# Reworked seams between the stages of a decoder layer, and one more down group by block products

## The chip, the cores and the metric

The kernel runs on one core of a Trainium2 chip. The metric is the device time of one execution in microseconds (us). A core has TensorE (matrix products; PE in the profile, its weight loads PEld), VectorE (DVE), ScalarE (ACT), GpSimd (POOL) and SyncE (SP). The engines run their own instruction queues in order and wait for each other by semaphores; the sequencers of SP, ACT and POOL also issue the transfers (DMA) between the large memory (HBM) and the on-chip memory (SBUF). TensorE adds its results up in PSUM, eight banks of 512 fp32 columns.

## The reference

One layer of a decoder trunk, 512 tokens, width 2048: a normed input goes through gated linear attention (GLA, four heads), then a squared-ReLU MLP of width 8192, then a sigmoid gate times a projection of a per-layer embedding, and a final norm. All in fp32.

```python
u = rmsnorm(h, norm_mix);   h = h + gla_mixer(u, ...)           # w_in, chunked recurrence, w_out
h = h + square(relu(rmsnorm(h, norm_mlp) @ w_up)) @ w_down      # 2048 -> 8192 -> 2048
gate = sigmoid(rmsnorm(h, norm_ple) @ w_ple_gate)
h = h + gate * (p @ w_ple_proj)
return rmsnorm(h, norm_final)
```

## The kernel before

**Products.** Every large product is done in split fp32: each operand is a high part in the fast format fp32r (a cast on ScalarE) and a low part (value minus high part, on VectorE), and a product is three matmuls, high*high, high*low and low*high (`mm3`, lines 147 to 151, or the same inside `chunk`, lines 819 to 822). Most of the kernel's matmuls take a stationary 128x128 tile and 512 moving columns.

**Stages in order of time.** The GLA input projections and the attention (to about 690 us), the output projection `wo` (to 840), the up product (to 1500), the embedding projection (to about 1545), the down product (to about 2237), the gate product and the final norm.

**Block products.** The up product and part of the down product use a scheme of seven block products instead of eight. Weights and activations are split in two along the contraction, and each again in halves (256 tokens, 128 columns); `chunk_sums` (line 796) loads 512 KB of weights into a buffer `raw` with eight places and forms three sums there with three VectorE operations (L801, L804, L805); `chunk` (line 808) then makes high parts (L811) and low parts (L813) of seven places at a time, twice, and runs 2 x 7 x 3 = 42 matmuls of 256 columns. `combine` (line 825) puts the seven results together from PSUM in a wide buffer `e` (tag "w", of which there is one) by one ScalarE copy and five VectorE operations. A plain chunk (`plain_chunk`, line 882) does the same 512 KB of weights with 4 x 2 x 3 = 24 matmuls of 512 columns, one cast and one subtraction.

**Up stage.** 32 groups g of 256 hidden columns, four chunks each (k4 = 0 to 3). After the first chunk of the next group, `hidden` (line 838) combines, applies relu and square on ScalarE (L840, L841) and stores the result to `z_d` by two transfers on GpSimd's queue (L843).

**Down stage.** The 32 row chunks come in five slices of 4, 3, 3, 3, 3 chunks. In every slice eight output groups g run over the slice's chunks and add their sum to the residual `h_d` (load L847, additions L861 or L892, store L855; in the last slice one more multiplication by `f2`, L854). Groups 0, 3 and 7 are plain, the others use block products. `build` (line 896) makes the operands of one chunk, twice: it loads a pair of hidden tiles from `z_d` into a load buffer, forms three differences (L872 to L874) in a spare tile, and splits both the tiles and the differences into four slots (L871, L875, L876, L877). It is called at a slice's group 0, chunk by chunk, and for one chunk of the next slice after group 2.

**Buffers.** `wpool` has tags raw (3 buffers: incoming weights, the `pp` tiles of the embedding projection, and `u_late`), whi and wlo (4 each) and ld (2). `spool` has 34 slots of 4 KB, which hold all operands; up operands take 28, a slice of three chunks 24. `mpool` has single buffers.

**Seams.** In the output projection, `evac_out` (line 731) adds the residual, scales it into `u`, squares it and stores it; for the pairs kp = 0 to 4 of 128-row blocks it also makes the up operands at once. For kp = 5 and 6 the scaled copy goes into `u_late`, a tile of tag raw, and the operands of 5, 6, 7 are made after the loop (line 756). Then the first up weights are summed (line 966). At the start of the down stage the embedding projection runs in four parts (`project_embedding`, line 932), each after a `build`.

**Order.** The program's order is only a priority: a planner in the compiler simulates the program and puts each instruction into its engine's queue when, by its own account, it is ready and its buffer is free. `keep_in_program_order` on L801 restricts that for the first weight sum. Weights are all loaded on SyncE's queue, and hidden tiles and residuals on GpSimd's.

## Time and profile before

| | |
|---|---|
| times of three runs | 2417.47, 2419.46, 2421.09 us, median 2419.46 |
| profiled execution | 2423.99 us, its span from first to last instruction 2422.2 us |
| TensorE busy | 2361.6 us (97%), weight loads 2136.3 us (88%) |
| VectorE, ScalarE, GpSimd busy | 1690.2 (70%), 977.5 (40%), 152.5 us (6%) |
| mean granted TensorE clock | 0.984 |
| DMA | 341.09 MB, mean 141 GB/s |
| chain that ended last | PE 78%, issue 8%, DVE 5%, DMA 4% |

The page's strip of 40 slices (60.6 us each) shows TensorE at 9 tenths or more except in the first slice (7), the one from 787 (8), the one from 1514 (8) and the last (8). Busy time of a pipelined matmul is modelled, so the step from one matmul's start to the next one's is the better measure of its cost.

### The profile page before, as it was taken

How to read it: one execution, taken by the hardware profiler on the slowest of the kernel's cores; microseconds unless marked ns; L12 is line 12 of the kernel's file. 1: busy time of each engine (PE TensorE's matmuls, PEld its weight loads, DVE VectorE, ACT ScalarE, POOL GpSimd, SP SyncE). 2: the span in 40 equal slices, each digit the busy share in tenths (PEclk: the TensorE clock that was granted, in tenths of full speed). 3: DMA queues.
4: the chain of work that ended last, by engine and by line, in shares of the span. 5: the costliest groups of instructions: out<-in, count | busy, mean ns of one | idle time of the engine just before them, and what ended most of it. 6: DMA issues, size and time to landing. Idle time of an engine off the chain costs nothing.

```text
span 2422.2 us, 36477 instructions
## 1 busy us (share of the span) xinstructions
PE 2361.6 (97%) x14778; PEld 2136.3 (88%) x14778; DVE 1690.2 (70%) x2579; ACT 977.5 (40%) x1216; POOL 152.5 (6%) x282
## 2 busy tenths in 40 slices
PE   7999999999999899999999999899999999999998
PEld 6888888888878699999999998699898989899887
DVE  5654736547464588888888888578887888878435
ACT  4433424324332344444444446334433334434333
POOL 2000000000000000000000000000101010100000
PEclk8999999999999899999999999899999999999999
DMA  8333323332433344444444444545555565655433
GB/s 252 97 88 94 87 79 96 95 94 85 127 130 113 122 124 146 132 131 131 132 131 131 131 131 142 184 149 170 191 179 195 187 203 178 215 191 190 149 114 113
DMA packets 247753, 341.09 MB, mean 141 GB/s; under 512 B 13732, under 2 KB 202336, under 8 KB 247584
## 3 DMA queue, kind: packets, MB, share of 16 engines
q1 hardware_dynamic: 213072, 228.68, 31.0%
q0 software_dynamic: 30240, 105.75, 12.6%
q10 hardware_dynamic: 4272, 4.33, 0.6%
q8 instruction: 115, 1.88, 0.3%
q14 instruction: 54, 0.44, 0.1%
HBM read 281.05 MB, written 57.67 MB: 140 GB/s over the span
## 4 chain that ended last, share of the span: by engine, by line
PE 78%; issue 8%; DVE 5%; DMA 4%; ACT 1%; POOL 0%; ACTq 0%; DVEq 0%; POOLq 0%
PE ps_up L822 9%; PE ps_up L819 9%; PE ps_up L821 9%; PE ps_d L821 5%; PE ps_d L819 5%; PE ps_d L822 4%; DMA z<-z_d 3%; PE ps_wo L151 2%; PE ps_v L149 2%; PE ps_wo L149 2%; PE ps_v L150 2%; PE ps_og L150 2%; PE ps_v L151 2%; PE ps_og L149 2%; PE ps_og L151 2%
## 5 line engine op out<-in xcount | busy, mean ns | idle before, releaser
L811 ACT CAST whi_up<-raw_up 128x896 fp32r<-128x896 f32 x256 | 239.8, 940 | 317.5 <-PE ps_up L821 309.5
L813 DVE TENSOR_TENSOR wlo_up<-raw_up,whi_up 128x896 fp32r<-128x896 f32 x256 | 277.7, 1087 | 92.9 <-ACT whi_up L811 92.9
L819 PE MATMUL ps_up<-XS,whi_up 128*128 128x256 f32 x1024 | 290.4, 284 | 0.0
L821 PE MATMUL ps_up<-XS,whi_up 128*128 128x256 f32 x1024 | 290.4, 284 | 0.0
L822 PE MATMUL ps_up<-XS,wlo_up 128*128 128x256 f32 x1024 | 290.0, 284 | 0.0
L811 ACT CAST whi_d<-raw_dn 128x896 fp32r<-128x896 f32 x160 | 149.0, 942 | 241.1 <-PE ps_d L821 141.8
L819 PE MATMUL ps_up<-XA,whi_up 128*128 128x256 f32 x768 | 218.6, 285 | 3.7 <-ACT whi_up L811 3.7
L822 PE MATMUL ps_up<-XA,wlo_up 128*128 128x256 f32 x768 | 218.1, 284 | 0.5 <-DVE wlo_up L813 0.5
L821 PE MATMUL ps_up<-XA,whi_up 128*128 128x256 f32 x768 | 217.8, 284 | 0.0
L813 DVE TENSOR_TENSOR wlo_d<-raw_dn,whi_d 128x896 fp32r<-128x896 f32 x160 | 172.9, 1087 | 35.6 <-ACT whi_d L811 34.8
L819 PEld LDWEIGHTS ps_up<-XS,whi_up 128*128 128x128 f32 x1024 | 197.4, 193 | 0.0
L821 PEld LDWEIGHTS ps_up<-XS,whi_up 128*128 128x128 f32 x1024 | 197.3, 193 | 0.0
L822 PEld LDWEIGHTS ps_up<-XS,wlo_up 128*128 128x128 f32 x1024 | 197.1, 193 | 0.0
L821 PE MATMUL ps_d<-Zdl,whi_d 128*128 128x256 f32 x640 | 181.1, 283 | 0.0
L819 PE MATMUL ps_d<-Zdh,whi_d 128*128 128x256 f32 x640 | 181.1, 283 | 0.0
L822 PE MATMUL ps_d<-Zdh,wlo_d 128*128 128x256 f32 x640 | 181.1, 283 | 0.0
L150 PE MATMUL ps_d<-Zl,whi_d 128*128 128x512 f32 x384 | 151.9, 396 | 5.0 <-DVE Zl L876 5.0
L149 PE MATMUL ps_d<-Zh,whi_d 128*128 128x512 f32 x384 | 151.7, 395 | 3.9 <-ACT whi_d L139 2.2
L151 PE MATMUL ps_d<-Zh,wlo_d 128*128 128x512 f32 x384 | 151.5, 394 | 0.5 <-DVE wlo_d L141 0.5
L819 PEld LDWEIGHTS ps_up<-XA,whi_up 128*128 128x128 f32 x768 | 147.9, 193 | 4.2 <-ACT whi_up L811 3.9
L822 PEld LDWEIGHTS ps_up<-XA,wlo_up 128*128 128x128 f32 x768 | 148.0, 193 | 0.9 <-DVE wlo_up L813 0.8
L821 PEld LDWEIGHTS ps_up<-XA,whi_up 128*128 128x128 f32 x768 | 148.0, 193 | 0.2 <-issue 0.2
(345 smaller groups left out, 6057.9 us busy)
## 6 DMA issues: line engine op xcount, KB each, us to landing
raw_up<-in_w_up SPq DMA_DIRECT2D x128, 512.0 KB, 3.8
raw_dn<-in_w_down SPq DMA_DIRECT2D x80, 512.0 KB, 3.7
raw_d<-in_w_down SPq DMA_DIRECT2D x48, 512.0 KB, 3.8
h<-h_d POOLq DMA_DIRECT2D x40, 512.0 KB, 4.6
h_d<-h POOLq DMA_DIRECT2D x40, 512.0 KB, 3.0
raw_v<-in_gla_w_in SPq DMA_DIRECT2D x32, 512.0 KB, 3.8
raw_og<-in_gla_w_in SPq DMA_DIRECT2D x32, 512.0 KB, 3.7
raw_wo<-in_gla_w_out SPq DMA_DIRECT2D x32, 512.0 KB, 3.4
```

The lines of the kernel that those rows point to most:

```text
L149: nc.tensor.matmul(ps, lhsT=wa[0], rhs=wb[0], start=first, stop=False)
L150: nc.tensor.matmul(ps, lhsT=wa[0], rhs=wb[1], start=False, stop=False)
L151: nc.tensor.matmul(ps, lhsT=wa[1], rhs=wb[0], start=False, stop=last)
L811: nc.scalar.copy(hi[:, 1:8, :], raw[:, q_, 1:8, :])
L813: nc.vector.tensor_tensor(out=lo[:, 1:8, :], in0=raw[:, q_, 1:8, :], in1=hi[:, 1:8, :].bitcast(F32), op=ALU.subtract)
L819: nc.tensor.matmul(dst, lhsT=hi[:, wb, :], rhs=xh, start=first and q_ == 0 and half == 0, stop=False)
L821: nc.tensor.matmul(dst, lhsT=hi[:, wb, :], rhs=xl, start=False, stop=False)
L822: nc.tensor.matmul(dst, lhsT=lo[:, wb, :], rhs=xh, start=False, stop=last and q_ == 1 and (b == 3 or half == 1))
```

## The change

- `PLAIN` becomes (0, 7): group 3 of every slice is done by block products.
- Up stage: after `hidden`, `hidden_sums` forms the four differences of the hidden tile in the free half of `e` and stores them to a new buffer in HBM, `zd_d`. The two steps are taken one per chunk (`todo.pop(0)()`), no longer both at once.
- Down stage: `split` loads hidden tiles, or their stored differences, straight into the slot of the low part, casts the high part from it and subtracts in place. `build_to` does this for the tiles and `build_sums_to` for the differences, at separate times: tiles of the next slice after groups 2 and 6, differences after group 7 and during group 1.
- The embedding projection's four parts stand behind the four plain chunks of the first slice's group 0, and its `pp` tiles use the load buffers, of which there is one more (tag "ld2").
- Output projection: the scaled copies of kp 5 and 6 are written over the residual tile after it is stored; no `u_late`. The first up weights are loaded and summed after block i = 13. Square and scaling change places.
- x is loaded one block earlier. `f2` shares the single buffer of `acc2`.

```diff
-PLAIN = (0, 3, 7)
+PLAIN = (0, 7)
...
+    zd_d = dram.tile([NG, P, 4, HT], F32, name="zd_d")
...
     x_load(1)
+    x_load(2)
...
-                if ready % 2 == 0 and ready // 2 + 1 < NK // 2:
-                    x_load(ready // 2 + 1)
+                if ready % 2 == 0 and ready // 2 + 2 < NK // 2:
+                    x_load(ready // 2 + 2)
...
+    def load2(shape, name):
+        return mpool.tile(shape, F32, tag="ld2", name=name)
...
+    def scale_out(i, h):
+        nc.vector.scalar_tensor_tensor(
+            out=late["u"][:, i % 2, :], in0=h, scalar=vec("norm_mlp", i), in1=rb, op0=ALU.mult, op1=ALU.mult)
...
-            late["x"] = load([P, 2, T], f"xres_{kp}")
+            late["x"] = (load2 if kp == 5 else load)([P, 2, T], f"xres_{kp}")
...
-            if kp == 5:
-                late["s"] = wtile([P, 2, 2, T], "raw", "u_late")
             if kp in (5, 6):
-                late["u"] = late["s"][:, kp - 5, :, :]
+                late["u"] = late["x"]
...
-        nc.vector.scalar_tensor_tensor(
-            out=late["u"][:, i % 2, :], in0=h, scalar=vec("norm_mlp", i), in1=rb, op0=ALU.mult, op1=ALU.mult)
         add_squares(h, f"mlp_{i}", i == 0)
+        if kp not in (5, 6):
+            scale_out(i, h)
         if i % 2:
             nc.gpsimd.dma_start(h_d[kp], late["x"])
+            if kp in (5, 6):
+                for j in range(2):
+                    scale_out(i - 1 + j, late["x"][:, j, :])
+            if i == 13:
+                first_raw.append(raw_of(0))
...
-        bcast(ft, f2, "f2")
+        F2.append(mpool.tile([P, T], F32, tag="acc2", name="f2"))
+        bcast(ft, F2[0], "f2")
...
+    def hidden_sums(g, e):
+
+        for o, x, y in ((4, 2, 3), (5, 3, 1), (6, 2, 5), (7, 0, 6)):
+            nc.vector.tensor_tensor(out=e[:, o, :], in0=e[:, x, :], in1=e[:, y, :], op=ALU.subtract)
+        nc.gpsimd.dma_start(zd_d[g], e[:, 4:8, :])
...
-    def hidden_operands(kp, u, d):
...
+    def split(src, kp, name):
+
+        h, l = (slot([P, 4, HT], f"Z{name}{n}_{kp}", F32R) for n in ("h", "l"))
+        nc.gpsimd.dma_start(l.bitcast(F32), src)
+        nc.scalar.copy(h, l.bitcast(F32))
+        nc.vector.tensor_tensor(out=l, in0=l.bitcast(F32), in1=h.bitcast(F32), op=ALU.subtract)
+        return h, l
...
     def build_to(n):
+
         while built[0] < min(n, NG // 2):
-            build(built[0])
+            for kp in (2 * built[0], 2 * built[0] + 1):
+                u = split(z_d[kp].rearrange("p k (h t) -> p (k h) t", h=2), kp, "u")
...
+    def build_sums_to(n):
+        while built[1] < min(n, NG // 2):
+            for kp in (2 * built[1], 2 * built[1] + 1):
+                d = split(zd_d[kp], kp, "d")
+                ZOPS[kp][:4] = [(d[0][:, o, :], d[1][:, o, :]) for o in range(4)]
+            built[1] += 1
...
-            o = wtile([P, 2, 512], "raw", f"pp_{gi}_{t2}")
+            o = (load2 if (2 * gi + t2) % 3 == 2 else load)([P, 2, 512], f"pp_{gi}_{t2}")
...
-    raw_next = raw_of(0)
+    raw_next = first_raw[0]
...
-            if s_ == 0 and g == 0 and first:
-                for i in range(4):
-                    build_to(i // 2 + 1)
-                    project_embedding(i)
             if g == 0:
                 build_to(k4 + 1)
+            if g == 1:
+                build_sums_to(k4 + 1)
...
                 plain_chunk(ps, k4, g, first, last, f"{name}_{k4}")
+                if s_ == 0 and g == 0:
+                    flush()
+                    build_to(min(k4 + 2, end))
+                    project_embedding(k4)
+                    build_sums_to(k4 + 1)
...
-            if g == 2 and last and 8 * (SLICES[s_] + 1) <= 34:
-                build_to(end + 1)
+            if last and end < NG // 2:
+                if g == 2 and SLICES[s_] == 3:
+                    build_to(end + 2)
+                if g == 6:
+                    build_to(end + 3)
+                if g == 7:
+                    build_sums_to(end + 1)
         if todo and not first:
-            flush()
+            todo.pop(0)()
```

## Rows read from the trace of the kernel before

**Rows 1.** Busy time by stretch (from:to, length, engines, granted clock, DMA share, GB/s).
```profile
45.00:60.00 15.00, 8.13 (x27) 5.73 (x26) 8.59 (x11) 7.18 (x21) 3.39 (x5) 0.66 0.72 215
785.00:800.00 15.00, 9.92 (x29) 7.19 (x28) 7.95 (x12) 4.15 (x6) 1.28 (x2) 0.66 0.41 139
840.00:855.00 15.00, 8.27 (x40) 7.67 (x39) 14.97 (x28) 6.78 (x10) 1.33 (x2) 0.66 0.33 105
1500.00:1550.00 50.00, 35.67 (x114) 26.13 (x113) 30.38 (x38) 26.68 (x34) 4.29 (x8) 0.80 0.64 212
1720.00:1740.00 20.00, 17.20 (x86) 14.32 (x85) 17.14 (x26) 7.56 (x8) 2.12 (x4) 0.91 0.49 174
```
**Rows 2.** TensorE in order of time (start us, us), a plain and a block-product group.
```profile
1557.08 0.39 PE L150 MATMUL ps_d<-Zl,whi_d 128*128 128x512 f32 x1
1557.31 0.39 PE L151 MATMUL ps_d<-Zh,wlo_d 128*128 128x512 f32 x1
...
1590.29 0.28 PE L819 MATMUL ps_d<-Zdh,whi_d 128*128 128x256 f32 x1
1590.41 0.28 PE L821 MATMUL ps_d<-Zdl,whi_d 128*128 128x256 f32 x1
```
**Rows 3.** SyncE's queue in order of time, 30 to 60 us.
```profile
33.22 14.87 SPq L137 DMA_DIRECT2D raw_v<-in_gla_w_in  x3
48.14 2.01 SPq L244 DMA_DIRECT2D x<-in_x  x3
```
**Rows 4.** SyncE's queue from 1478, and line 822 (first and last start us).
```profile
1480.34 44.25 SPq L137 DMA_DIRECT2D raw_wp<-in_w_ple_proj  x4
...
L822 PE MATMUL ps_up<-XA,wlo_up x12: 283/283/385, 1491.3 to 1500.4; 128*128 128x256 f32 x12
...
L822 PE MATMUL ps_d<-Zh,wlo_d x6: 283/283/283, 1570.0 to 1574.7; 128*128 128x256 f32 x6
```
**Rows 5.** ScalarE in order of time, 785 to 792 us.
```profile
790.81 1.99 ACT L139 CAST whi_wo<-raw_wo 128x1024 fp32r<-128x1024 f32 x2
```
**Rows 6.** VectorE in order of time, 838 to 845 us (idle before in brackets).
```profile
839.61 1.37 DVE L745 TENSOR_TENSOR xres<-ps_wo,xres 128x512 f32<-128x512 f32 x2 [10.06 <-PE ps_wo L151]
...
844.82 0.68 DVE L801 TENSOR_TENSOR raw_up<-raw_up 128x512 f32<-128x512 f32 x1
```
**Rows 7.** TensorE in order of time, 843 to 848 us.
```profile
847.86 0.58 PE L819 MATMUL ps_up<-XA,whi_up 128*128 128x256 f32 x1 [2.60 <-ACT whi_up L811]
```
**Rows 8.** VectorE in order of time in the last slice, 2183 to 2188 us.
```profile
2183.64 0.68 DVE L834 TENSOR_TENSOR e_dn<-ps_d,e_dn 128x512 f32<-128x512 f32 x1
2184.24 0.41 DVE L835 TENSOR_TENSOR e_dn<-ps_d,e_dn 128x256 f32<-128x256 f32 x1
2184.57 1.28 DVE L861 TENSOR_TENSOR h<-h,e_dn 128x512 f32<-128x512 f32 x2
2185.78 1.08 DVE L813 TENSOR_TENSOR wlo_d<-raw_dn,whi_d 128x896 fp32r<-128x896 f32 x1
2186.78 1.22 DVE L854 TENSOR_TENSOR h<-h,f 128x1024 f32<-128x1024 f32 x1
2187.91 0.69 DVE L801 TENSOR_TENSOR raw_dn<-raw_dn 128x512 f32<-128x512 f32 x1
```
**Rows 9.** An up group's wide buffer by engine; transfers (KB, us to landing).
```profile
992.67 0.37 ACT L829 COPY e_up<-ps_up 128x256 f32<-128x256 f32 x1
...
1000.27 1.14 POOL L843 DMA_DIRECT2D z_d<-e_up  x2 [19.01 <-ACT e_up L841]
...
z_d<-e_up POOLq DMA_DIRECT2D x64, 256.0 KB, 2.8
...
h_d<-xres POOLq DMA_DIRECT2D x8, 512.0 KB, 2.9
```
**Rows 10.** Lines that write acc2 and read f2 (ns min/median/max, first to last start us).
```profile
L1037 DVE TENSOR_TENSOR acc<-acc,sq_ple x15: 683/685/694, 2136.7 to 2252.2; 128x512 f32<-128x512 f32 x15
...
L854 DVE TENSOR_TENSOR h<-h,f x8: 1218/1218/1224, 2117.9 to 2237.7; 128x1024 f32<-128x1024 f32 x8
```

More of the change, by code (lines that the diff above doesn't have):

```diff
@@ L725, in operands, with chunk_sums, raw_of @@
         return ops
+    w_up = a["w_up"].rearrange("o k c -> (o k) c")
+    w_dn = a["w_down"].rearrange("o k c -> (o k) c")
+    B11, T1, T3, B22, B21, T2, T4 = range(1, 8)
+    PRODUCTS = ((A11, B11), (R2, T2), (S3, T3), (S1, T1), (A12, B21), (R4, B22), (A22, T4))
+    BANK = ((0, 0), (0, 1), (1, 0), (1, 1), (2, 0), (2, 1), (3, 0))
+    def chunk_sums(w, k4, g, name):
+        raw = wtile([P, 2, 8, P], "raw", f"raw_{name}")
+        rows = raw.rearrange("p q (k b n) c -> p (q k) b (n c)", k=2, b=2)
+        nc.sync.dma_start(rows[:, :, 0, :], w_rows(w, 4 * k4, 4, 256 * g, 256))
+        tc.keep_in_program_order(nc.vector.tensor_tensor(
+            out=raw[:, :, 2:4, :], in0=raw[:, :, 1:5:3, :], in1=raw[:, :, 0:1, :].broadcast_to([P, 2, 2, P]),
+            op=ALU.add))
+        nc.vector.tensor_tensor(out=raw[:, :, 6, :], in0=raw[:, :, 2, :], in1=raw[:, :, 4, :], op=ALU.add)
+        nc.vector.tensor_tensor(out=raw[:, :, 7, :], in0=raw[:, :, 6, :], in1=raw[:, :, 5, :], op=ALU.add)
+        return raw
+    work = []
+    for g in range(NG):
+        for k4 in range(NK // 4):
+            work.append((0, g, k4, k4 == 0, k4 == NK // 4 - 1))
+    c0 = 0
+    for s_, nc_ in enumerate(SLICES):
+        for g in range(NKP):
+            for j in range(nc_):
+                work.append((1 + s_, g, c0 + j, j == 0, j == nc_ - 1))
+        c0 += nc_
+    def raw_of(n):
+        if n >= len(work):
+            return None
+        stage, g, k4, _, _ = work[n]
+        if stage == 0:
+            return chunk_sums(w_up, k4, g, f"up{g}_{k4}")
+        if g not in PLAIN:
+            return chunk_sums(w_dn, k4, g, f"dn{g}_{k4}")
     late = {}
     XOPS = [None] * NKP
+    first_raw = []
+    def scale_out(i, h):
+        nc.vector.scalar_tensor_tensor(
+            out=late["u"][:, i % 2, :], in0=h, scalar=vec("norm_mlp", i), in1=rb, op0=ALU.mult, op1=ALU.mult)
     def evac_out(i, ps):
@@ L835, in combine @@
         nc.vector.tensor_tensor(out=e[:, 1, :], in0=ps[3][:, 0, :], in1=e[:, 6, :], op=ALU.subtract)
[L836 removed]
+        return e, e[:, 0:4, :].rearrange("p (f h) t -> p f (h t)", f=2)
     def hidden(g, ps):
[L839 removed]
+        e, z = combine(ps, f"up{g}")
         nc.scalar.activation(out=z, in_=z, func=AF.Relu)
@@ L893, in add_plain @@
         residual_out(s_, g, hs)
-    built = [0]
-    def build(kc):
-        for kp in (2 * kc, 2 * kc + 1):
-            u = load([P, 2, T], f"z_{kp}")
-            nc.gpsimd.dma_start(u, z_d[kp])
-            d = spare_tile([P, 4, HT], f"zd_{kp}")
-            hidden_operands(kp, u, d)
+    built = [0, 0]
     def build_to(n):
         while built[0] < min(n, NG // 2):
-            build(built[0])
-            built[0] += 1
+            for kp in (2 * built[0], 2 * built[0] + 1):
+                u = split(z_d[kp].rearrange("p k (h t) -> p (k h) t", h=2), kp, "u")
+                ZOPS[kp] = [None] * 4 + [(u[0][:, o, :], u[1][:, o, :]) for o in (0, 2, 3)]
+                for k in range(2):
+                    ZH[2 * kp + k] = [t[:, 2 * k:2 * k + 2, :].rearrange("p h t -> p (h t)") for t in u]
+            built[0] += 1
+    def build_sums_to(n):
[4 more added lines that the diff above has]
+            built[1] += 1
     todo = []
@@ L943, in project_embedding @@
                 pp_d[2 * t2:2 * t2 + 2, :, 512 * gi:512 * gi + 512].rearrange("t p c -> p t c"), o)
-    work = []
-    for g in range(NG):
-        for k4 in range(NK // 4):
-            work.append((0, g, k4, k4 == 0, k4 == NK // 4 - 1))
-    c0 = 0
-    for s_, nc_ in enumerate(SLICES):
-        for g in range(NKP):
-            for j in range(nc_):
-                work.append((1 + s_, g, c0 + j, j == 0, j == nc_ - 1))
-        c0 += nc_
-    def raw_of(n):
-        if n >= len(work):
-            return None
-        stage, g, k4, _, _ = work[n]
-        if stage == 0:
-            return chunk_sums(w_up, k4, g, f"up{g}_{k4}")
-        if g not in PLAIN:
-            return chunk_sums(w_dn, k4, g, f"dn{g}_{k4}")
-    raw_next = raw_of(0)
+    raw_next = first_raw[0]
     ps = None
```

50 lines of the change are left out of this document (11 added, 39 removed).

## The prediction

> **What bounds the kernel now.** I read the page's first two parts, then a table of stretches, then the queues of single engines. TensorE is busy for 97% of the span and the page's second part shows full slices except at the start, around 790 to 850 and around 1500. So the kernel is bound by TensorE, and a change can gain only by giving it fewer columns or by closing the places where it stands still or runs at half clock. The reader is to see in [rows 1] five such places. I price each as the idle time of TensorE plus its busy time multiplied by what the granted clock lacks (the two levels are 1.2 and 2.4 GHz, 0.5 and 1.0 in the column):
>
> - 45 to 60: 15 - 8.13 = 6.9, and 8.13 x 0.34 = 2.8: 9.6 us lost.
> - 785 to 800: 5.1 + 9.92 x 0.34 = 8.5 us.
> - 840 to 855: 6.7 + 8.27 x 0.34 = 9.5 us.
> - up to down: the last matmul of line 822 in the up stage starts at 1500.4, its first in the down stage at 1570.0 [rows 4]. Between them stand 96 projection and 96 plain matmuls of 512 columns, 192 x 0.227 = 43.5 us by the step of [rows 2]. Of 69.6 us, 26 are lost. The table of 1500 to 1550 sees 14.3 + 35.67 x 0.20 = 21.5 of it.
> - 1720 to 1740 [rows 1]: 2.8 + 17.2 x 0.09 = 4.4 us, and the next slice boundary at 1850 repeats it: 8.8 us for two (the last two are under 1 us each).
>
> Together 62 us, 2.6% of the span.
>
> **The change part by part.**
>
> *Group 3 by block products.* The steps of TensorE from start to start are 0.227 us for 512 columns and 0.120 us for 256 [rows 2]. A plain chunk is 24 x 0.227 = 5.45 us, a chunk of seven products 42 x 0.120 = 5.04 us. Sixteen chunks (4 + 3 + 3 + 3 + 3) change: 16 x 0.41 = 6.5 us gained on the path. What it adds is VectorE work: three weight sums and two low parts instead of one low part, and five combines per group. VectorE overlaps its neighbours, so I take steps from start to start [rows 8]: low part 1.00, 512-column operation 0.60, 256-column 0.33, an addition to the residual 0.60 each, the final scaling 1.13, the wide weight sum 0.69 less the overlap of 0.08. A chunk is 0.61 + 0.66 + 2.00 = 3.27, a group of three 9.8 + 2.2 (combine) + 1.2 = 13.2 against 15.1 of TensorE, 14.4 in the last slice. Six such groups now follow each other where a plain one gave relief. By steps it fits; if every instruction cost its full duration (3 x 3.7 + 2.6 + 1.4 + 1.2 = 16.3) the last slice would lose 6 x 1.2 = 7.3 us. I take 0, nearest to the steps, and keep 7.
>
> *u_late no longer in a weight buffer (785 to 800).* One of three raw buffers is held by it from 787 on. The weights of the next group had landed, but their two casts stand in ScalarE's queue behind the cast of u_late and start at 790.81 [rows 5]. In the page's second part the slices of the earlier output groups, with three buffers, are full. I expect the hole gone: 8 us. The new cost: the scaled copy is written in place, so it waits for the store of the residual (issue 0.57, landing 2.9 [rows 9]), twice. Queued behind it on VectorE is at worst a low part of the output weights; buffers of low parts hold four chunks, so nothing follows on TensorE. If that cover is gone the gain is 8.5 - 2 x 3.5, about 1.5.
>
> *First weight sums of the up stage moved before the end of the output projection (840 to 855).* Before, VectorE idles for 10.06 us until the last output matmul, then does the last residual and operands, and starts the first weight sum only at 844.82 [rows 6]; the first up matmul comes at 847.86 [rows 7]. In the changed kernel chunk 0 is summed, cast and split in that idle time, and TensorE has 5.0 us of work at 840. Next late is chunk 1: its sums still follow the last operands, some 1.6 us (one chunk's sums, 0.61 + 0.66, and a wait) sooner than now, so ready at about 847 where chunk 0 ends at 845. I leave 3.5 us: gain 6. From the other side 2 (only the sums' own time) to 9.5.
>
> *Sums stored in the up stage.* Per group four VectorE operations of 256 columns (4 x 0.33 = 1.3) and one store on GpSimd's queue. VectorE has 4 x 3.27 + 2.2 + 1.3 = 16.6 of 42 x 4 x 0.120 = 20.2 us: hidden, 0. The store keeps the one wide buffer e longer, which is the third rival.
>
> *Up to down.* Before, the eight pp tiles share the three raw buffers with the weights: SyncE holds the four projection loads for 44.25 us [rows 4], and each pair of operands costs a load buffer, three differences and two splits before a plain chunk can go. Now pp uses load buffers, operands land in their own slots, and a plain chunk stands between two projections, so weights for 5.45 us of matmuls arrive per 512 KB. Removed from VectorE: three differences, 0.60 + 0.33 + 0.33, a pair. What is late next is DMA: from about 1485 to 1562 I count 44 transfers of 0.52 MB (8 hidden, 8 sums, 8 projection stores, 11 down weights, 4 projection weights, 5 residual and hidden stores), 23 MB in 77 us or 298 GB/s. The row of 1500 to 1550 moves 212 GB/s at a share of 0.64, so a full share would be about 330. It fits with 10% to spare, and a weight load may be late by two chunks before TensorE notices. I leave 5 us: gain 21, from 12 (half closed) to 26.
>
> *Operands of later slices earlier.* Hidden operands are now asked for after group 2 and 6 and their sums after group 7, beside 15 us groups, instead of at the boundary. Slots suffice: 24 held, 8 more, of 34. Gain 8 of 8.8; 4 if one of the two loads stays late.
>
> *x one load earlier.* SyncE holds three v weight loads for 14.87 us while three x loads wait behind them until 48.14 [rows 3]; the stretch 45 to 60 pays. If each x load takes the place of the one before, one of the three goes ahead of the block and TensorE has some 6 us more to do. But the order is set by the planner, and x loads that go first also delay weights. I take 4, between 9.6 and -4.
>
> *f2 in the buffer of acc2.* The squares of the last norm now wait for the last scaling with f2 (2237.7), where they started at 2136.7 [rows 10]. Sixteen squares and 15 additions, about 10 us, must fit beside the first gate group, 192 matmuls of 0.227 = 43.5 us. 0; at most 10.
>
> *GpSimd's queue.* 64 more transfers are issued there. Two hidden stores take 1.14 us with VectorE at work [rows 9], so 0.57 each. That is 0.57 x 64 = 36 us of issuing, spread over two long stages in which the queue waits most of the time: 0.
>
> **The sum.** 6.5 + 8 + 6 + 21 + 8 + 4 = 53.5 us. The profiled execution took 2424.0 us (span 2422.2); 2424.0 - 53.5 = 2370.5. The median of the runs shown is 4.5 us under the profiled one, so I forecast 2366 us.
>
> **The rivals.**
>
> 1. *Half comes back.* The holes are moved, not closed: DMA is the bound of the long seam, x stays where it is, the boundaries keep one late load, the last slice waits for VectorE. 6 + 4 + 12 + 4 + 0 + 3 = 29 us: 2390. For it: the planner sets the order and I cannot see its new order; 298 of 330 GB/s is tight. Against: each hole has a named cause that the change removes.
> 2. *All of it closes*, x included: 9.6 + 8.5 + 9.5 + 26 + 8.8 + 6.5 = 69 us: 2351. Against it is that chunk 1 and the transposes of the embedding remain.
> 3. *The wide buffer becomes the bound: slower.* e is taken at 992.67; the stores are issued at 1000.27, 1.14 for two, and land 2.8 later [rows 9]: 11.5 us of a group's 20.2. With the sums right behind the square it would be held for 7.6 + 1.3 + 0.6 + 2.9 = 12.4 (the landing is that of the residual's store of the same size); one chunk of 5.04 later 17.4; two chunks later 22.5. In the last case each of 31 groups waits 2.3 us: 2366 + 71 = 2437. It decides from a hold of 20.2, and the sign turns at 21.9. Against it: VectorE has 3.5 us of a group free, so the sums should not fall that far behind. The rows also show that a store issued from GpSimd takes 0.57 us with VectorE at work. The Trainium skill (SBUF — State Buffer, section "SBUF: two separate sides") says that such a transfer is starved of descriptors while VectorE runs an operation in a mode that takes both ports, about 620 ns becoming about 3100. By that rule the three stores of a group would cost some 7.5 us more, an estimate from the page's two figures, and with the sums one chunk late the buffer would be held for 24.9 and the time be 2366 + 31 x 4.7 = 2512; the rows show no such stretching, so I give this 0.01 of the rival's chance.
> 4. *The change does not do what it says*: loads keep their places since slots or the planner's order hold them, and only the block products count, with the hole at 785 closed: 6.5 + 8 = 15 us, 2405. For it speaks that loads which wait for nothing already sit behind others at the start [rows 3]; against it that the u_late edit is no matter of order.
>
> **How the numbers follow.** Forecast 0.58, half 0.22, all 0.11, wide buffer 0.04, no use 0.05. The forecast's own range, half the way to the first two rivals, is 2358 to 2378. The range 2347 to 2402 takes in the first two rivals and the high ends of all terms; the low ends all at once (6.5 - 7 + 1.5 + 2 + 12 + 4 - 4 - 10 = 5 us, 2415), the wide buffer and most of the fourth lie outside, about 0.12. A difference under 0.2%, 5 us, cannot be told from none here. Faster 0.94 (the first three and 0.03 of the fourth), same 0.02, slower 0.04.
>
> **What would show it.** TensorE full at 785 to 800 with no cast of output weights late; first up matmul within 1 us of the last output matmul; between the last up matmul and the first block product of the down stage some 48 us instead of 69.5; no dip at slice boundaries; 16 plain chunks fewer. Wrong: a periodic hole in the up stage (wide buffer), idle before low parts in the last slice (VectorE), a DMA share near 1 around 1500 with TensorE waiting for weights.

## The result, and the profile after

The changed kernel takes 2387.24 us (median of 4, 2385.63 to 2390.76) against 2420.28 for the kernel before on the same chip: a ratio of 0.9866, 95% interval 0.9849 to 0.9883. Timed again beside other kernels it was 0.9874 (0.9854 to 0.9893). About 33 us are gained, 37 in the two profiled spans (2422.2 and 2385.2), where 53.5 were forecast. The sign and the range held; the forecast's own range, 2358 to 2378, did not.

To see where the time went, I count TensorE from the start of each matmul to the start of the next and call lost what is above the step at full speed (columns / 2.4 GHz + 13.4 ns, which gives the 0.227 and 0.120 of [rows 2]). That takes in both standing still and half clock; the rest is work. Lost time falls from 125.7 to 95.3 us and work from 2283.7 to 2277.3, together 36.8 of the 37.0; the rest of each span, 12.8 and 12.6 us, lies before the first matmul and after the start of the last.

| place (us in the trace of before) | lost before | lost after | forecast gain | gain |
|---|---|---|---|---|
| work: group 3 by block products | | | 6.5 | 6.4 |
| start, 0 to 80 | 28.2 | 29.0 | 4 | -0.8 |
| attention to output projection, 640 to 680 | 4.4 | 9.8 | not seen | -5.4 |
| middle of the output projection, 780 to 800 | 8.9 | 0 | 8 | 8.9 |
| output projection to up, 830 to 870 | 12.0 | 4.5 | 6 | 7.5 |
| up to down, 1480 to 1560 | 27.5 | 12.6 | 21 | 14.9 |
| starts of the later slices | 11.0 | 2.9 | 8 | 8.1 |
| inside the last slice | 0.9 | 3.7 | 0 | -2.8 |
| all else | 32.8 | 32.8 | 0 | 0 |

Each row compares one trace with one trace. Most places repeat within about 1 us from trace to trace; the seam from up to down does not, as the experiments show.

Stretches of the changed kernel, with the columns of [rows 1]:

```profile
20.00:30.00 10.00, 3.85 (x11) 2.38 (x10) 1.40 (x4) 2.41 (x8) 0.74 (x1) 0.50 0.88 249
45.00:60.00 15.00, 13.04 (x62) 10.06 (x61) 6.87 (x8) 6.48 (x14) 6.16 (x11) 1.00 0.73 209
640.00:660.00 20.00, 16.36 (x85) 13.95 (x83) 9.25 (x15) 5.99 (x12) 4.45 (x8) 0.99 0.36 120
785.00:800.00 15.00, 15.00 (x68) 12.43 (x67) 7.04 (x10) 4.08 (x5) 0.56 (x1) 1.00 0.44 140
840.00:855.00 15.00, 12.99 (x108) 12.70 (x108) 14.62 (x34) 7.34 (x11) 0.00 (x0) 1.00 0.43 133
1500.00:1550.00 50.00, 43.13 (x193) 35.47 (x193) 28.52 (x33) 27.33 (x37) 9.45 (x18) 0.93 0.88 324
1510.00:1520.00 10.00, 6.99 (x23) 5.03 (x22) 5.07 (x5) 6.57 (x9) 1.06 (x2) 0.83 1.04 416
2120.00:2130.00 10.00, 7.99 (x65) 7.59 (x63) 9.83 (x17) 4.00 (x6) 1.59 (x3) 1.00 0.66 225
```

The kernel before in two stretches that [rows 1] does not have:

```profile
20.00:30.00 10.00, 10.00 (x41) 7.97 (x40) 5.92 (x10) 6.24 (x19) 1.86 (x3) 0.74 0.77 246
640.00:660.00 20.00, 19.95 (x105) 17.11 (x103) 13.20 (x25) 8.88 (x15) 3.23 (x6) 1.00 0.42 132
```

Against [rows 1], 785 to 800 is full, 840 to 855 stands still for 2 us instead of 6.7, and 45 to 60 for 2 instead of 6.9. But 20 to 30, full before at a clock of 0.74 (2.6 us lost as idle and clock), is now 6.15 us idle and at half clock, and 640 to 660, full before, stands still for 3.6. At 1500 to 1550 the DMA share went from 0.64 to 0.88. In 2120 to 2130 VectorE is busy for 9.83 of 10 us.

Three queues name the new waits. First ScalarE at the start (start us, us, engine, line, operation; in brackets idle before and what ended it); the same load had been issued at 10.6 and was used at 21 before the change:

```profile
13.62 0.40 ACTq L327 DMA_DIRECT2D lr_raw<-in_gla_w_in  x1
...
28.27 1.29 ACT L335 CAST lr_w<-lr_raw 128x128 fp32r<-128x128 f32 x6 [7.51 <-DMA lr_raw<-in_gla_w_in]
```

Then GpSimd at the seam to the output projection: the load of xres_5 (line 785) stands 31 us at the head of the queue, for a matmul of the attention stage, with the last ten of the twelve loads of gated behind it:

```profile
654.30 0.74 POOL L785 DMA_DIRECT2D xres<-xT_d  x1 [31.18 <-PE ps_o L615]
655.04 2.68 POOL L597 DMA_DIRECT2D gr<-gated_d  x5
```

TensorE there, waiting for ScalarE, which needs those loads:

```profile
660.02 1.22 PE L150 MATMUL ps_wo<-GH,whi_wo 128*128 128x512 f32 x2 [3.65 <-ACT GH L602]
```

The long seam. Line 855 has the low parts of block products; its last matmul of the up stage starts at 1489.0 and the first block product of the down stage (line 852) at 1541.2, 52.2 us where [rows 4] have 69.6, and where the prediction's sign was "some 48". The transfers of 1500 to 1530 (the profile's DMA view: fortieths of the stretch, then median us from issue to landing):

```profile
DMA  9998738969999999999999999999999999999999
GB/s 324 369 373 246 60 83 238 243 228 392 414 425 412 408 427 400 426 412 421 407 412 418 418 423 421 421 397 389 419 415 403 419 395 381 416 380 370 400 384 370
...
pp_d<-pp ACTq DMA_DIRECT2D x6, 512.0 KB, 9.0
Zdl<-zd_d POOLq DMA_DIRECT2D x5, 512.0 KB, 12.5
...
raw_dn<-in_w_down SPq DMA_DIRECT2D x2, 512.0 KB, 10.1
```

DMA is full for 25 us and a weight load takes 10 us to land where the page has 4.0 over the whole span. GpSimd's queue shows why the operand loads come in one bunch, and why two come late:

```profile
1499.83 1.11 POOL L876 DMA_DIRECT2D z_d<-e_up  x2 [19.91 <-ACT e_up L874]
...
1503.17 1.14 POOL L910 DMA_DIRECT2D Zul<-z_d  x2
...
1533.16 0.53 POOL L887 DMA_DIRECT2D h<-h_d  x1 [19.41 <-DMA pp_d<-pp]
1533.76 1.12 POOL L910 DMA_DIRECT2D Zdl<-zd_d  x2
```

For 20 us the z store of the last up group stands at its head; then twelve operand loads and stores start within 14 us; then a residual load stands for 19 us until the store of a projection (pp) lands and frees its buffer, with two loads of sums behind it.

### The profile page after: what moved, and what is told of

Read it like the earlier page. It is cut to its first block, busy times and chain, and to the rows that moved or that the text cites. A ratio compares the mean times of both kernels' runs of the same rounds, so it can differ in the third digit from the quotient of the medians.

```text
span 2385.2 us, 37471 instructions
## 1 busy us (share of the span) xinstructions
PE 2338.2 (98%) x15066; PEld 2133.8 (89%) x15066; DVE 1734.0 (73%) x2700; ACT 987.5 (41%) x1237; POOL 186.6 (8%) x346
## 4 chain that ended last, share of the span: by engine, by line
PE 83%; issue 6%; DMA 5%; DVE 4%; ACT 1%; POOL 0%; ACTq 0%; SPq 0%; POOLq 0%; DVEq 0%
PE ps_up L855 9%; PE ps_up L854 9%; PE ps_up L852 9%; PE ps_d L855 6%; PE ps_d L852 6%; PE ps_d L854 6%; PE ps_v L150 2%; PE ps_v L152 2%; PE ps_v L151 2%; PE ps_og L150 2%; PE ps_og L151 2%; PE ps_og L152 2%; PE ps_wo L150 2%; PE ps_wo L152 2%; PE ps_wo L151 2%
## 5 line engine op out<-in xcount | busy, mean ns | idle before, releaser
L844 ACT CAST whi_d<-raw_dn 128x896 fp32r<-128x896 f32 x192 | 177.0, 941 | 261.1 <-DVE raw_dn L747 118.0
L846 DVE TENSOR_TENSOR wlo_d<-raw_dn,whi_d 128x896 fp32r<-128x896 f32 x192 | 207.6, 1086 | 16.7 <-ACT whi_d L844 15.2
L852 PE MATMUL ps_d<-Zdh,whi_d 128*128 128x256 f32 x768 | 217.7, 283 | 0.0
L854 PE MATMUL ps_d<-Zdl,whi_d 128*128 128x256 f32 x768 | 217.6, 283 | 0.0
L855 PE MATMUL ps_d<-Zdh,wlo_d 128*128 128x256 f32 x768 | 217.4, 283 | 0.0
L852 PE MATMUL ps_d<-Zuh,whi_d 128*128 128x256 f32 x576 | 163.6, 284 | 4.7 <-ACT whi_d L844 4.7
L855 PE MATMUL ps_d<-Zuh,wlo_d 128*128 128x256 f32 x576 | 164.2, 285 | 3.8 <-DVE wlo_d L846 3.4
L854 PE MATMUL ps_d<-Zul,whi_d 128*128 128x256 f32 x576 | 163.3, 284 | 0.0
L852 PEld LDWEIGHTS ps_up<-XA,whi_up 128*128 128x128 f32 x768 | 147.4, 192 | 2.2 <-ACT whi_up L844 1.9
L852 PEld LDWEIGHTS ps_d<-Zdh,whi_d 128*128 128x128 f32 x768 | 147.8, 192 | 0.0
```

Of the source, the lines that this page charges most:

```text
L844: nc.scalar.copy(hi[:, 1:8, :], raw[:, q_, 1:8, :])
L846: nc.vector.tensor_tensor(out=lo[:, 1:8, :], in0=raw[:, q_, 1:8, :], in1=hi[:, 1:8, :].bitcast(F32), op=ALU.subtract)
L852: nc.tensor.matmul(dst, lhsT=hi[:, wb, :], rhs=xh, start=first and q_ == 0 and half == 0, stop=False)
L854: nc.tensor.matmul(dst, lhsT=hi[:, wb, :], rhs=xl, start=False, stop=False)
L855: nc.tensor.matmul(dst, lhsT=lo[:, wb, :], rhs=xh, start=False, stop=last and q_ == 1 and (b == 3 or half == 1))
```

## The experiments

Theory: the steps were right where an engine's work was counted, and the 16.7 us that did not come (53.5 less 36.8) went to four places: loads that stand ahead of others in GpSimd's queue (640 to 680), a load pushed back at the start, a DMA peak at the seam, VectorE in the last slice. The rival to each is in its expectation. All ratios are to the kernel before, timed beside them.

**One load put back in its place.**

```
-            nc.gpsimd.dma_start(late["x"], ...)
+            (tc.keep_in_program_order if kp == 5 else id)(nc.gpsimd.dma_start(late["x"], ...))
```

> The changed kernel with one load put back in its program place: that of the sixth residual pair (xres_5, line 785) stands behind the 16 loads of gated on GpSimd's queue instead of ahead of eight of them. Lost time is idle time of TensorE plus busy time times what the granted clock lacks. In the changed kernel 640 to 680 loses 6.2 us (before the change 1.1); the load waited 31 us for the last matmul of line 615 at 654.3, since its new buffer lies over memory of the attention stage. Theory (the load blocks the queue): ScalarE's wait for gr (8.7 us) and the hole around 657 go, 640 to 680 loses about 1 us again and the time falls by 4 to 6 us, to about 2382. Rival (the gated loads wait for something else, or ScalarE and the attention's last outputs set that point): the hole stays within 1 us and the time is 2387 within 2.

Ratio 0.9841 (0.9828 to 0.9855), 2385.33 us; that is 6 to 8 us less than the changed kernel's two ratios give, with intervals that overlap a little. Only GpSimd's order differs from the changed kernel (the expectation miscounts the loads: ten of twelve stood behind this one). Its loads of gated now start at 653.43, and the stretches of this kernel are full again:

```profile
640.00:660.00 20.00, 20.00 (x106) 17.46 (x105) 12.84 (x20) 8.61 (x15) 3.23 (x6) 1.00 0.46 145
660.00:680.00 20.00, 18.93 (x77) 13.61 (x77) 15.03 (x31) 9.27 (x15) 0.00 (x0) 1.00 0.18 57
```

640 to 680 loses 4.8 us by my count instead of 9.8: the theory holds and gives the row of 5.4 its cause. The span fell by only 1.3 us, though, as the seam from up to down, with the same instructions in the same order, lost 16.6 us in this trace instead of 12.6. Over the five traces that have these instructions in this order (the changed kernel twice, this kernel and the next two) it lost from 12 to 18 us.

**The start: the low-rank load first, or the x loads put back.**

```
+    x_load(0); lr_raw = slot(...); nc.scalar.dma_start(lr_raw, w_in[...])      # first kernel; its old place removed
...
-    x_load(2)                                                                  # second kernel
-                if ready % 2 == 0 and ready // 2 + 2 < NK // 2: x_load(ready // 2 + 2)
+                if ready % 2 == 0 and ready // 2 + 1 < NK // 2: x_load(ready // 2 + 1)
```

> The changed kernel with the 16-column low-rank weights (lr_raw) loaded at the very start instead of after the first chunk. In the changed kernel this load was issued at 13.6 and landed at about 28, among x loads and weights at a DMA share of 0.88 to 0.95, and TensorE stood for 6.15 us before ps_lr (20 to 30 loses 6.15 + 3.85 x 0.5 = 8.1 us, before the change 2.6). Theory (the earlier x loads push lr_raw back, and that is where the gain at 45 to 60 went): the wait for lr_w goes, 20 to 30 loses 2 to 3 us and the time falls by 4 to 6 us, to about 2382. Rival (DMA as a whole is the limit of the first 40 us, so the next load, x or weights, is late by as much): the hole moves behind 30 and the time is 2387 within 2.

> The changed kernel with only the x loads put back by one place, as before the change. Theory (the shift moved a hole and closed none): 45 to 60 loses about 9.6 us again (now 2.0), 20 to 30 about 2.6 (now 8.1), and the time is 2387 within 2. Rival (the prediction's step: one x load earlier is worth 4 us): the time rises by 4 to 2391 or more. Should it fall by more than 2 us, the shift was a loss.

Low-rank first: 0.9816 (0.9802 to 0.9829), 2379.93 us. X loads put back: 0.9849 (0.9835 to 0.9862), 2387.09. Stretches of the first:

```profile
20.00:30.00 10.00, 10.00 (x52) 8.03 (x52) 7.83 (x13) 8.14 (x26) 2.55 (x4) 1.00 0.94 309
45.00:60.00 15.00, 13.52 (x70) 10.63 (x69) 10.21 (x15) 8.90 (x30) 3.33 (x7) 1.00 0.65 217
```

and of the second:

```profile
20.00:30.00 10.00, 9.96 (x43) 7.85 (x42) 7.55 (x12) 7.21 (x22) 1.24 (x3) 0.86 0.73 231
45.00:60.00 15.00, 7.78 (x33) 6.08 (x34) 7.58 (x11) 6.50 (x22) 2.90 (x5) 0.77 0.73 227
```

0 to 80 loses 17.9 us with the low-rank load first and 29.0 in the changed kernel: the late load was the cause, and it was worth 11 us by this count (12 to 14 by the ratios), twice what the theory gave it. With the x loads back the hole stands at 45 to 60 again and 0 to 80 loses 26.2, about as before (28.2). So the shift alone only moved a hole, at a cost of 1 to 3 us by this count (4 to 6 by the ratios, with intervals that overlap). What the prediction wanted of the shift comes once lr_raw is out of the way: the start then loses 7 to 10 us less than before the change (17.9 here, 20.7 in the four-edit kernel below). Without the shift 20 to 30 loses only 0.04 + 9.96 x 0.14 = 1.4 us, so the low-rank load is late only with it; that load first and no shift was not run.

**The last up group's stores issued by ScalarE.**

```
-            nc.gpsimd.dma_start(z_d[g, :, f, :], z[:, 1 - f, :])
+            (nc.scalar if g == NG - 1 else nc.gpsimd).dma_start(z_d[g, :, f, :], z[:, 1 - f, :])
...
-        nc.gpsimd.dma_start(zd_d[g], e[:, 4:8, :])
+        (nc.scalar if g == NG - 1 else nc.gpsimd).dma_start(zd_d[g], e[:, 4:8, :])
```

> The changed kernel with the three stores of the last up group (two of z, one of the sums) issued by ScalarE instead of GpSimd. In the changed kernel GpSimd's queue stands from 1479.4 to 1499.8 with the z store of the last group at its head, and behind it are the loads of operands whose slots come free from 1485 on; then 12 transfers start between 1499.8 and 1513 and DMA is full (share 0.98 to 1.04 in 1505 to 1530) while TensorE loses 6.9 + 43.1 x 0.07 = 9.9 us in 1500 to 1550. Theory (queue order bunches the transfers): the loads go out from 1485 on, the peak of DMA is lower, and 1500 to 1550 loses 4 us or less; the time falls by 4 to 7 us, to about 2381. Rival (DMA has too much to move in this stretch in any order, or the weights wait for their raw buffers): the loss stays within 2 us of 9.9 and the time within 2 of 2387.

0.9889 (0.9876 to 0.9903), 2397.10 us: 4 to 6 us slower than the changed kernel by its two ratios, with intervals that overlap. The seam from 1460 to 1560 lost some 21 us, more than in any of the five traces above, so neither theory nor rival held. The loads went out from 1481 as hoped, and 1500 to 1530 lost 2.0 us; but then one hole of 13 us came. GpSimd's queue in this kernel, and ScalarE's behind it:

```profile
1490.21 0.53 POOL L910 DMA_DIRECT2D Zul<-z_d  x1 [1.57 <-PE ps_up L855]
1530.76 0.53 POOL L887 DMA_DIRECT2D h<-h_d  x1 [40.01 <-DMA pp_d<-pp]
1531.35 0.54 POOL L910 DMA_DIRECT2D Zdl<-zd_d  x1
...
1541.63 0.53 POOL L887 DMA_DIRECT2D h<-h_d  x1 [7.01 <-DMA pp_d<-pp]
1542.23 0.53 POOL L910 DMA_DIRECT2D Zdl<-zd_d  x1
```

```profile
1541.32 1.04 ACT L911 CAST Zdh<-Zdl 128x1024 fp32r<-128x1024 f32 x1 [2.74 <-DMA Zdl<-zd_d]
1547.40 1.04 ACT L911 CAST Zdh<-Zdl 128x1024 fp32r<-128x1024 f32 x1 [5.04 <-DMA Zdl<-zd_d]
1550.07 1.78 ACT L844 CAST whi_d<-raw_dn 128x896 fp32r<-128x896 f32 x2 [1.63 <-DVE raw_dn L747]
```

VectorE between these two casts:

```profile
1548.48 1.22 DVE L912 TENSOR_TENSOR Zdl<-Zdl,Zdh 128x1024 fp32r<-128x1024 f32 x1 [1.53 <-ACT Zdh L911]
```

A residual load stands 40 us for the store of a projection, and four loads of sums stand behind it and its like. Their casts stand in ScalarE's queue, and their low parts (line 912) in VectorE's. Behind such a low part stands the last sum of the first block products' weights (line 747, at 1549.62). The cast of these weights waits for that sum, and TensorE for the cast. That gave the next theory.

**Residual loads in program order, alone and with the stores.**

```
-        nc.gpsimd.dma_start(hs, h_d[g])
+        (tc.keep_in_program_order if s_ == 0 and g < 3 else id)(nc.gpsimd.dma_start(hs, h_d[g]))
```

> The changed kernel as it is, as the measure for the runs beside it, and to see how far the seam from up to down repeats itself: the runs so far with the same instructions there (the changed kernel and those with the sixth residual load, the low-rank load or the x loads moved) lost 12 to 18 us between 1460 and 1560 from trace to trace. Theory (the seam depends on how transfers happen to meet, as DMA is full there): the seam loses another amount within 11 to 18 us, with the holes in other places. Rival (the differences come from the edits): it loses 12.6 us as before, within 1. Ratio to the kernel before 0.9866 within 0.0015 in either case.

> The changed kernel with the residual loads (line 887) of the first three groups of the first slice put back in their program place, so that the last two of the sums' loads (line 910) no longer stand behind one of them. In the changed kernel GpSimd's queue stands 19.4 us, to 1533.2, with the residual load h_2 at its head (it waits for the load buffer of a pp tile whose store must land), and the last two loads of sums go out at 1533.8 and 1534.4; ScalarE then waits for them with the casts of the first block products' weights behind it. Where the stores of the last group were moved to ScalarE, all four stood behind such loads (40 us at the head of the queue) and one hole of 13 us came of it. Theory (head of line on GpSimd's queue): 1530 to 1550 loses 1 us or less instead of 6, the seam falls by 4 to 6 us and the time with it, ratio to the changed kernel 0.998. Rival (DMA is full until 1530 and the loads would only land later): the loads go out earlier and land after 1535 all the same; time and seam within 2 us.

> Both edits: residual loads in program order, and the three stores of the last up group issued by ScalarE. Alone, the second cost about 6 us, since its 13 us hole at 1537 to 1550 outweighed what it gave at 1510 (1500 to 1530 lost 2 us there, in the changed kernel 5.2). Theory (both holes come from what stands at the head of GpSimd's queue): with the residual loads out of the way the hole at 1540 goes too, the seam from 1460 to 1560 loses 4 to 6 us and the time is 7 to 9 us below the changed kernel. Rival (ScalarE, with three issues and a wait for the sums more, sets that seam): 1500 to 1560 still loses over 9 us, within 3 us of the changed kernel.

The changed kernel again: 0.9874, and its seam lost 14.3 us instead of 12.6. Residual loads in order: 0.9869 (0.9845 to 0.9893). With the stores: 0.987 (0.985 to 0.989). Neither differs from the changed kernel; their seams lost 12.3 and 13.6, within the spread. Both theories failed. The two loads of sums did go out at 1516 and 1518 instead of 1534 and landed 6 to 8 us earlier, but TensorE's hole at 1540 stayed (2.46 us, as in the changed kernel). That 1530 to 1540 lost nothing is no gain of this edit: the changed kernel run again lost nothing there either. ScalarE in the kernel with the residual loads in order:

```profile
1536.49 0.59 ACT L978 COPY pp<-ps_ple 128x512 f32<-128x512 f32 x1 [4.65 <-PE ps_ple L152]
...
1542.00 1.78 ACT L844 CAST whi_d<-raw_dn 128x896 fp32r<-128x896 f32 x2
...
1548.13 1.05 ACT L911 CAST Zuh<-Zul 128x1024 fp32r<-128x1024 f32 x1 [3.40 <-DMA Zul<-z_d]
1549.08 1.78 ACT L844 CAST whi_d<-raw_dn 128x896 fp32r<-128x896 f32 x2
```

Now the weights' cast (line 844) stands behind the copies of the projections, and its next one behind a cast of operands for the next slice (Zuh), whose load (Zul) stands behind a residual load that waits 23 us for a projection's store.

**Four edits together.** Low-rank load first, xres_5 and the residual loads in order, and the accumulator of the gate's squares in a buffer of its own (`acc2 = load2([P, T], "acc3")`).

> The changed kernel with four edits in four places: low-rank weights first, the sixth residual pair's load in its program place, the residual loads of the first slice in theirs, and the accumulator of the gate's squares in a load buffer that has come free instead of the one it shares with f2. The first gave 11 us at the start by the trace (0 to 70 lost 17.7 instead of 29), the second 5 at 640 to 680. Theory (four separate causes, which add): 11 + 5 + 5 + 1.7 (2230 to 2240 lost 2.0 us, before the change 0.3), the time falls by 18 to 23 us, to a ratio of 0.977 to the kernel before; 2230 to 2240 loses under 0.5 us. Rival (the seam takes back what comes earlier, and the gate's 2 us are its own): 10 to 13 us, ratio 0.981.

0.9807 (0.9786 to 0.9827), 2373.10 us beside 2390.02 of the changed kernel: the fastest of all, 17 us below the changed kernel and 46 below the one before. Its span is 15.6 us shorter than that of the changed kernel run beside it; by place: start 8.3 better, 640 to 680 about 6, seam 4, slices 2 to 3 worse, gate 0. That is a little under the theory's 18 to 23 us and over its rival's 10 to 13. The 4 us of the seam lie within its spread. What was taken back was taken by the slices, and it goes with the residual loads: 1600 to 2000 loses 5.0 to 6.2 us in the three kernels that have them in program order, and 2.1 to 3.2 in the five traces without. So that edit, which showed no gain at the seam, cost some 3 us later; the other three edits without it were not run. The edit to the accumulator did nothing: 2.06 us are lost there in this kernel and 2.05 in the kernel before (2260 to 2280), and my "0.3 before" was read at the wrong place.

**u_late back in a raw buffer.**

```
-                late["u"] = late["x"]
+                late["s"] = wtile([P, 2, 2, T], "raw", "u_late") if kp == 5 else late["s"]; late["u"] = late["s"][:, kp - 5, :, :]
```

(and each half is scaled at once).

> The changed kernel with u_late back in a raw weight buffer, scaled at once instead of in place after the store. All else is as changed. Theory (that buffer made the hole): 785 to 800 (some us later or earlier) loses 8 us again, where the changed kernel loses nothing, and the time rises by 6 to 8 us, to a ratio of 0.990 to the kernel before. Rival (the hole closed because the first sums of the up stage or other weights now stand differently in the queues): it stays closed and the ratio is 0.987.

0.9901 (0.9885 to 0.9916), 2396.52 us: 6 to 9 us slower than the changed kernel (the interval is clear of its first one and overlaps the second), and 9.0 us are lost at 790 to 810, where the changed kernel loses none. ScalarE and TensorE there; the casts stand behind u_late's as in [rows 5]:

```profile
797.09 0.40 ACT L724 CAST XA<-u_late 128x256 fp32r<-128x256 f32 x1
797.40 1.99 ACT L140 CAST whi_wo<-raw_wo 128x1024 fp32r<-128x1024 f32 x2
```

```profile
798.50 0.79 PE L150 MATMUL ps_wo<-GH,whi_wo 128*128 128x512 f32 x1 [4.09 <-ACT whi_wo L140]
```

**Block products alone**, on the kernel before: `PLAIN = (0, 7)`. It keeps that kernel's choice of banks (`g not in (1, 5)`), by which groups 2, 3 and 4 each take both banks of the smaller pool; the changed kernel lets odd and even groups alternate.

> The kernel before with group 3 of the down stage by seven block products and nothing else of the change. Theory (16 chunks of 42 steps of 0.120 us in place of 24 of 0.227, VectorE keeps up): 6.5 us less, ratio 0.9973. Rival (six such groups in a row leave VectorE behind in the last slice, where each group also scales the residual, and the slice boundaries lose a relief): 0 to 3 us less, ratio 0.999 to 1.000, with TensorE waiting for VectorE in the last slice.

1.0039 (1.0026 to 1.0052), 2428.95 us: slower than before, which neither theory nor rival had. Work falls by 6.4 us as computed, but the down stage after its first slice loses 25.9 us, 11.9 in the kernel before. Its waits of TensorE (engine, line, waited for: us in all, times, longest):

```profile
PE ps_d L819 <- DVE e_dn L835: 3.3, 3, 1.8
PE ps_d L819 <- ACT whi_d L811: 3.0, 3, 1.4
...
PE ps_d L822 <- DVE wlo_d L813: 1.9, 4, 0.6
```

None of these three stands in the trace of before. VectorE's combine (line 835) holds the banks, and VectorE is busy for 36.9 of 40 us at 2010 to 2050, where the kernel before has 31.7. So on the kernel before this term does not pay. Three things of the change can make it pay: banks that alternate, operands that VectorE no longer has to form from three differences, and loads before the boundary. Which of them does was not tested, and neither was the changed kernel with group 3 plain again. In the changed kernel the same view has 4.2 us, all of it VectorE's in the end, as ScalarE (line 844) waited for VectorE's sums there:

```profile
PE ps_d L855 <- DVE wlo_d L846: 2.8, 3, 1.3
PE ps_d L852 <- ACT whi_d L844: 1.4, 1, 1.4
```

**Two tries at the rest of the seam**, both on the four-edit kernel. First the block products' first weights are asked for after the last plain ones:

```
-    raw, raw_next = raw_next, raw_of(n + 1)
+    raw, raw_next = raw_next, (None if (stage, g, last) == (1, 0, True) else raw_of(n + 1))
...
+                    raw_next = raw_of(n + 1) if last else raw_next     # after the last projection
```

Then two projections go to the first group of block products:

```
-                    project_embedding(k4)
+                    project_embedding(k4) if k4 < 2 else None
...
+                project_embedding(k4) if (s_, g) == (0, 1) and k4 in (2, 3) else None     # after that group's chunk
```

> The kernel with four edits (ratio 0.9807; its seam loses 10.2 us from 1460 to 1540), and the first weights of the block products (raw_dn) asked for after those of the last plain chunk and the last projection instead of ahead of them. In the four-edit kernel raw_dn is loaded at 1485 and holds one of three raw buffers to the end of the projections. Theory (a raw buffer less makes plain and projection weights late while DMA is full): the seam loses 4 to 6 us less, ratio 0.9785. Rival (DMA is full with the operands, and the weights would be late in any buffer; the block products then start later): no gain, or 1 to 3 us worse, ratio 0.981 to 0.982.

> The kernel with four edits (ratio 0.9807), with the last two of the four projections of the embedding moved from the plain group into the first group by block products. Theory (the seam's rest is that operands, projections and plain weights all move in the same 40 us, with DMA at a share of 1.0 for 20 to 30 us of them): two projections less take 3 MB out of it, the seam's loss falls by 4 us or more, ratio 0.979. Rival (the operands alone fill DMA when they are asked for together, and plain chunks without a projection between them want their weights faster: 5.45 instead of 10.9 us a chunk): the loss stays within 2 us of 10 or grows, ratio 0.981 or more.

Raw later: 0.9837 (0.9823 to 0.9850); projections spread: 0.9823 (0.9809 to 0.9836). Neither gains. The first is some 7 us worse than the four-edit kernel (intervals touch), more than its rival had. ScalarE and VectorE of the first, before TensorE's hole of 9.65 us that ends at 1534.43:

```profile
1532.14 1.04 ACT L911 CAST Zuh<-Zul 128x1024 fp32r<-128x1024 f32 x1 [4.85 <-DMA Zul<-z_d]
1533.44 1.78 ACT L844 CAST whi_d<-raw_dn 128x896 fp32r<-128x896 f32 x2 [0.25 <-DVE raw_dn L747]
```

```profile
1530.91 1.23 DVE L889 TENSOR_TENSOR h<-h,g 128x1024 f32<-128x1024 f32 x1 [1.57 <-DMA h<-h_d]
```

Again a cast of the next slice's operand (Zuh), late by its load, stands ahead of the weights. But that cast is not the last wait: the weights' own sums stand behind the scaling of the residual (line 889) in VectorE's queue and end at 1533.4. Both loads, the operand's and the residual's, come from the same place: the residual load stood 22.7 us, to 1526.2, for a projection's store, with the operand's behind it. In the second try the DMA share of 1490 to 1520 falls from 1.00 to 0.88 as meant, and TensorE stands still for 5.9 us of it instead of 2.9. It waits 2.9 us there for an operand of the plain chunks (Zuh) and 2.1 for the first weights of the block products (whi_d): without a projection between them the chunks come due sooner, as the rival had it, though its reason named the weights alone.

## Why the prediction was right or wrong

*Block products*: work 6.4 of 6.5, exact. That VectorE costs 0 was wrong: the last slice loses 2.8 us more. ScalarE's 6.74 us of idleness for the sums, and VectorE without a gap before:

```profile
2123.22 2.62 ACT L844 CAST whi_d<-raw_dn 128x896 fp32r<-128x896 f32 x3 [6.74 <-DVE raw_dn L747]
```

```profile
2120.76 1.29 DVE L743 TENSOR_TENSOR raw_dn<-raw_dn 128x512 f32<-128x512 f32 x2
2121.97 0.76 DVE L746 TENSOR_TENSOR raw_dn<-raw_dn 128x256 f32<-128x256 f32 x2
2122.64 0.76 DVE L747 TENSOR_TENSOR raw_dn<-raw_dn 128x256 f32<-128x256 f32 x2
```

The sum by steps (14.4 us of VectorE against 15.1 of TensorE in the last slice) left 0.7 us a group, and left out that the gate's operands (lines 1053 and 1054) are formed in the same stretch. The upper bound of 7 held. This is read from the trace; no run took VectorE work out of the last slice.

*u_late*: right in size (8.9 for 8) and in cause, shown by putting it back. But "queued behind it" was asked only of VectorE. The new load buffer (ld2) is in a pool that opens where the attention's pools close, so its first load waits for that stage's last matmul (line 615), and it moved ahead of ten others on GpSimd's queue. That cost 5.4 us at 640 to 680, and the term *GpSimd's queue: 0* is where it belonged: the issuing is indeed hidden (GpSimd is busy 34 us more, and 880 to 1460 loses nothing), but a queue that is served in order costs by what stands at its head.

*First weight sums*: 7.5 for 6. The first up matmul starts at 837.30, one step (0.23 us) after the last of the output projection (before at 847.86 [rows 7]). Chunk 1 is what is late next, as said: TensorE waits 1.8 us for its cast at 845.1.

*Sums in the up stage*: 0, right, and with it rival 3 falls. The buffer e is taken at 1022.72; its stores in the up stage:

```profile
1030.31 1.14 POOL L876 DMA_DIRECT2D z_d<-e_up  x2 [17.02 <-ACT e_up L874]
1032.90 0.54 POOL L883 DMA_DIRECT2D zd_d<-e_up  x1 [1.46 <-DVE e_up L882]
```

The last lands at 1038.0, so e is held for 15.3 us of 20.2. Each store took 0.54 to 0.57 us to issue, and those of z landed in a median 2.6 us (2.8 before), with VectorE busy for 73% of the span. The Trainium skill's rule of starved descriptors (SBUF — State Buffer, section "SBUF: two separate sides", about 3100 ns instead of 620) does not show here. The rule is for VectorE operations in a mode that takes both ports, and no run here tells whether these operations are in it, so the rows do not speak against the rule either.

*Up to down*: the step that failed most, 14.9 for 21 (bounds 12 to 26); with the seam's spread from trace to trace the gain is 10 to 15. "DMA is late next" was right, "fits with 10% to spare" was not, and in an odd way: the mean was as computed (the eight tens of 1480 to 1560 move 285 GB/s on average, 298 were estimated) and a full share moved more than the 330 that I scaled up. But the transfers come in a bunch that the order of GpSimd's queue makes, and the mean says nothing of that. What stays is no single wait: with the bunch spread (stores on ScalarE) or the residual loads put back, the next wait in the same chain (projection store, load buffer, residual load, operand load, operand cast and low part, weight sum and cast) took its place. With the same instructions in the same order the seam lost 12 to 18 us in five traces, so a difference of up to 5 us there says nothing. Which order would free the last 10 us stays open; a load buffer for the residual alone was not tried.

*Slices*: 8.1 for 8. *x*: -0.8 for 4, inside its bounds (9.6 to -4); "x loads that go first also delay weights" was the fear, and the load that was delayed is the low-rank one, which the prediction did not look at; moved first, it gave 11 us. *f2*: 0, right.

Of the gains only that of *u_late* was taken back by a run; those of the first weight sums, the seam and the slices are read from the traces, where they stand at the places that the change touches.

Rival 1 (2390) came nearest to the time, and three of its four parts are what happened: DMA at the seam, x, VectorE in the last slice. In part its time is luck: it had the slices at 4 for 8.1, the first sums at 4 for 7.5 and the seam at 12 for 14.9, all too low, and the 5.4 us lost at 640 to 680, which no rival had, took part of that back. Its 0.22 was too little: the forecast had taken each term at its named cause alone.

## What to carry to other kernels

Before a buffer is added, ask which load the planner can now issue sooner and what stands behind it on its queue: a load that waits at the head of an in-order queue costs more than its own transfer. A mean DMA rate under the limit does not show that transfers fit; list them by the moment their queue lets them go. And an edit's worth depends on what stands beside it: by the traces, block products gained some 3.6 us here (6.4 less 2.8), and alone, on the kernel before, they lost 0.4%.

## What the runs showed of the hardware

At a share of 1.04 DMA moved 395 to 416 GB/s over 20 us (1510 to 1530), with peaks of 427, where 330 had been scaled up from a share of 0.64 at 212 GB/s: share and rate are not proportional. The Trainium skill (Perfetto Trace Analysis, section "Roofline") says that a single active core is bounded by its 16 DMA engines at about 435 GB/s; with 416 in the fullest 10 us these runs agree. Half a megabyte that lands in a median 3.4 to 4.6 us over the whole span took a median 8.2 to 12.7 there.

The wait for the low-rank load cost a little more than its length. In 20 to 30 the granted clock was 0.50, the lower level, beside 6.15 us of standing still. It had fallen before that wait, in 15 to 20 (0.78 there), where TensorE stood still for 3.50 us to 18.95. It stayed low to about 35 (0.51 in 30 to 35), where the kernel before had 0.98 in 25 to 30 already. In all, 20 to 40 loses 11.3 us by my count and 4.0 before, so 7.3 more for a wait of 6.15.
